# Second MLP of a two-layer decoder trunk: normed input and 512-column products from the twelfth output tile on; attention: matmul bursts of a pair merged with the next pair's

## The chip, the cores and the metric

The kernel runs on one NeuronCore of one Trainium2 chip. It is a single program. The metric is the device time of one execution in microseconds (us); lower is better. Everything is float32; many matrix products take operands in a rounded float32 format that the kernel calls F32R and that TensorE streams faster.

## The reference, cut to what matters

```python
# D_MODEL = 1024, SEQ = 256, BATCH = 1, H = 16 heads of 64, D_FF = 4096, two layers
for i in range(2):
    sh1, sc1, g1, sh2, sc2, g2 = split(silu(c) @ w_mod[i] + b_mod[i], 6)
    h = rmsnorm(x, norm_mix[i]) * (1 + sc1) + sh1
    y = pool_mixer(h) if i == 0 else moba_attention(h)   # one key block here: causal attention + bias
    x = x + g1 * y
    h = rmsnorm(x, norm_mlp[i]) * (1 + sc2) + sh2
    x = x + g2 * (relu(h @ w_up[i]) ** 2) @ w_down[i]
return rmsnorm(x, norm_final)
```

rmsnorm(x, g) is x * R * g, with R one number for each of the 256 positions.

## The kernel before, in words

**Layout.** Activations are kept transposed: a tile is 128 features by S = 256 positions, and x is eight such tiles `xs[k]`. A weight matrix is cut into 128x128 tiles; `w_all` in HBM holds all of them in the order of use, 16 to a chunk of 1 MB.

**Products in two parts.** Each weight tile is split into a rounded high part and the remainder: ACT (ScalarE) makes `w_hi` (`split_hi`, line 248, 128x1024 for eight tiles, a *half*), then DVE (VectorE) makes `w_lo` = raw - high (`split_lo`, line 258). Activations are split in the same way. A product is high x high + high x low + low x high. `mm_sum` (lines 277 to 279) does it in three matmuls of 256 or 258 columns. `mm_wide` (lines 270 and 271) does it in two: one of 512 columns, with high and low of the activation side by side, and one of 256, and leaves two half sums in one PSUM bank, 256 columns each, that have to be added.

**Steps.** PE (TensorE) takes one weight tile in a step. `next_tile` first runs what `later(d, fn)` put down for this step, then, at every eighth step, splits the half that is AHEAD = 3 halves ahead. Each engine works strictly in the order in which instructions were issued this way. The second MLP's halves are w96 to w127; at its step 8h half w(96+h+3) is split, so w105 is for output tile 9 and w107 for output tile 11.

**The second MLP's first product** (`up(1, raws, R)`, tiles named m1u0 to m1u31, 256 steps). The norm factor R comes only after the sub-layer has begun, so the input is not normed: `unnormed` makes x times gain, split, in tiles `h11_raw` with two more columns that hold the shift, and the products are 258 columns wide. Behind the product, `unnormed_out` (lines 471, 473) multiplies by R and adds up the two extra columns into a bias, both on DVE; then ACT does Relu with that bias (738), the square is on DVE for the first four outputs (740) and on ACT after that (742), ACT makes the high part (758), and DVE the low part seven steps later (762). The first four outputs are worked on together (32 steps, k first), each later one takes eight steps. R is made from the norm's sums at step 18 (`norm_tail`, N3_AT) and is there at about step 28 (`to_sbuf`, line 429). The second product of an MLP (`down`, m0d and m1d) uses `mm_wide` for seven of its eight outputs.

**Attention.** Eight pairs of heads. A pair p has three outputs of the qkv product, eight steps each; beside those run, at steps set by `later`: `scores` (tiles sc, line 976), then on DVE the logits, on ACT exp (1002) and `normalize` (line 1013, tiles L), then on PE three transposes for each head (`transposes`, tiles pt, line 1019), two transposes of the values (`values`, tile pv, line 1029) and the products with them (`outputs`, tile po, lines 1043, 1044). A burst of these stands between two steps of the qkv product.

## Time and profile before

| | |
|---|---|
| median of 3 runs | 544.37 us (544.1 to 544.8) |
| the profiled execution | 544.81 us, of which the span from first to last instruction is 543.0 us |
| busy: PE, weight loads, DVE, ACT | 532.2, 494.2, 413.2, 323.9 us |
| qkv product with attention beside it, first start of a qkv matmul to that of the next product (wo) | 232.7 to 324.0 us |
| wo product | 324.0 to 349.7 us |
| second MLP, first product (m1u) | 349.7 to 444.1 us |
| second MLP, second product (m1d) | 444.1 to 534 us |
| HBM read | 138.64 MB |

A row of the timeline gives start and duration in us, engine, source line, operation, output<-inputs, their shapes and the count; in brackets stands the idle time of the engine ahead of it and who ended it. A row of groups gives busy time in us and the mean of one in ns. "Released by" is inferred from semaphores. In the chain of waits the time of a piece reaches to the start of the next piece, so there it is the true spacing of matmuls, while a matmul's own duration (280 ns) overlaps the next one's.

### The profile page before, as it was taken

What the parts mean: (1) busy time and instruction counts of PE and PEld (TensorE: products, weight loads), DVE (VectorE), ACT (ScalarE), POOL (GpSimd) and SP (SyncE); (2) the same over time, 40 slices, a digit from 0 to 9 for tenths busy, and PEclk for the clock granted to TensorE, in tenths of its full rate; (3) what the DMA queues carried; (4) which work ended last, traced back from release to release, by engine and by line L of the source; (5) the groups of instructions that cost most, each with busy time, mean ns of one, the idle gap of its engine ahead of it and who ended that gap; (6) DMA issues with size and microseconds to landing.
All of it is one profiled execution on the core that took longest, in us unless ns stands there. A gap on an engine that the chain in (4) does not pass through costs nothing.

```text
span 543.0 us, 10968 instructions
## 1 busy us (share of the span) xinstructions
PE 532.2 (98%) x4412; PEld 494.2 (91%) x4412; DVE 413.2 (76%) x837; ACT 323.9 (60%) x606; POOL 2.5 (0%) x18
## 2 busy tenths in 40 slices
PE   8899999999999999999999999999999999999995
PEld 7777999999988888999998999999999998888895
DVE  2857997899889889857999983876887786775542
ACT  4225336788644545447987777657987874445531
POOL 1000000000000000000000000000000000000000
PEclk9999999999999999999999999999999999999998
DMA  8999998488899989964467774444565467676002
GB/s 331 422 415 418 419 416 313 156 308 320 314 381 406 364 304 336 341 238 148 185 236 298 278 275 156 156 156 156 185 215 198 179 237 281 211 273 240 0 1 77
DMA packets 22338, 140.41 MB, mean 259 GB/s; under 512 B 2416, under 2 KB 4736, under 8 KB 5904
## 3 DMA queue, kind: packets, MB, share of 16 engines
q1 hardware_dynamic: 22048, 138.61, 68.1%
q10 hardware_dynamic: 144, 1.05, 0.5%
q8 instruction: 34, 0.56, 0.4%
q14 instruction: 16, 0.13, 0.1%
q0 software_dynamic: 96, 0.06, 0.0%
HBM read 138.64 MB, written 1.07 MB: 257 GB/s over the span
## 4 chain that ended last, share of the span: by engine, by line
PE 92%; DMA 6%; DVE 1%; ACT 0%; issue 0%; DVEq 0%; ACTq 0%
PE m1d L270 10%; PE m0d L270 9%; PE m1u L277 6%; PE m1u L278 6%; PE m1u L279 6%; PE m0u L277 5%; PE m0u L279 5%; PE m0u L278 5%; PE m1d L271 5%; PE m0d L271 5%; PE qkv L277 5%; PE qkv L278 4%; PE qkv L279 4%; DMA raw_c_sh<-in_w_mod 3%; DMA raw_c_g<-in_w_mod 2%; PE wo L277 1%
## 5 line engine op out<-in xcount | busy, mean ns | idle before, releaser
L258 DVE TENSOR_TENSOR w_lo<-raw_w,w_hi 128x1024 fp32r<-128x1024 f32 x160 | 194.6, 1223 | 59.7 <-ACT w_hi L248 58.0
L248 ACT CAST w_hi<-raw_w 128x1024 fp32r<-128x1024 f32 x159 | 165.4, 1047 | 78.1 <-PE m1d L270 25.0
L270 PE MATMUL m1d<-m1u_al,w_hi 128*128 128x512 f32 x224 | 78.7, 394 | 0.0
L270 PE MATMUL m0d<-m0u_al,w_hi 128*128 128x512 f32 x224 | 78.1, 392 | 0.0
L301 DVE SCALAR_TENSOR_TENSOR raw_m<-raw_m,cact 128x1024 f32<-128x1024 f32 x64 | 77.6, 1217 | 0.0
L277 PE MATMUL m1u<-h_raw,w_hi 128*128 128x258 f32 x256 | 72.8, 284 | 0.0
L278 PE MATMUL m1u<-h_raw,w_hi 128*128 128x256 f32 x256 | 72.6, 284 | 0.0
L279 PE MATMUL m1u<-h_raw,w_lo 128*128 128x258 f32 x256 | 72.5, 283 | 0.0
L277 PE MATMUL m0u<-h,w_hi 128*128 128x256 f32 x248 | 69.8, 281 | 0.0
L279 PE MATMUL m0u<-h,w_lo 128*128 128x256 f32 x248 | 69.6, 281 | 0.0
L278 PE MATMUL m0u<-h,w_hi 128*128 128x256 f32 x248 | 69.4, 280 | 0.0
L271 PE MATMUL m1d<-m1u_al,w_lo 128*128 128x256 f32 x224 | 63.0, 281 | 0.0
L271 PE MATMUL m0d<-m0u_al,w_lo 128*128 128x256 f32 x224 | 62.8, 280 | 0.0
L277 PE MATMUL qkv<-h_raw,w_hi 128*128 128x258 f32 x192 | 57.4, 299 | 0.0
L278 PE MATMUL qkv<-h_raw,w_hi 128*128 128x256 f32 x192 | 54.5, 284 | 0.0
L279 PE MATMUL qkv<-h_raw,w_lo 128*128 128x258 f32 x192 | 54.4, 283 | 0.0
L270 PEld LDWEIGHTS m1d<-m1u_al,w_hi 128*128 128x128 f32 x224 | 42.1, 188 | 9.8
L270 PEld LDWEIGHTS m0d<-m0u_al,w_hi 128*128 128x128 f32 x224 | 42.0, 188 | 9.5
L279 PEld LDWEIGHTS m1u<-h_raw,w_lo 128*128 128x128 f32 x256 | 48.8, 191 | 0.0
L277 PEld LDWEIGHTS m1u<-h_raw,w_hi 128*128 128x128 f32 x256 | 48.7, 190 | 0.0
L278 PEld LDWEIGHTS m1u<-h_raw,w_hi 128*128 128x128 f32 x256 | 48.5, 190 | 0.0
L277 PEld LDWEIGHTS m0u<-h,w_hi 128*128 128x128 f32 x248 | 46.7, 188 | 0.6 <-issue 0.4
(189 smaller groups left out, 984.7 us busy)
## 6 DMA issues: line engine op xcount, KB each, us to landing
raw_w<-in_w_all SPq DMA_DIRECT2D x79, 1024.0 KB, 5.6
raw_m<-in_w_mod SPq DMA_DIRECT2D x32, 1024.0 KB, 6.4
raw_c_sh<-in_w_mod SPq DMA_DIRECT2D x8, 1024.0 KB, 14.1
raw_c_g<-in_w_mod SPq DMA_DIRECT2D x4, 1024.0 KB, 12.4
raw_c_mlp<-in_w_mod SPq DMA_DIRECT2D x2, 1024.0 KB, 11.6
raw_c_shift<-in_w_mod SPq DMA_DIRECT2D x2, 1024.0 KB, 9.1
T<-bd SPq DMA_DIRECT2D x8, 256.0 KB, 8.3
x<-in_xT ACTq DMA_DIRECT2D x1, 1024.0 KB, 5.7
```

The lines of the kernel that those rows point to most:

```text
L248: nc.scalar.copy(hi, raw)
L258: nc.vector.tensor_sub(lo, raw, hi.bitcast(F32))
L270: nc.tensor.matmul(b, hi, hl[:, : 2 * S], start=start, stop=False)
L271: nc.tensor.matmul(b[:, S:], lo, hl[:, :S], start=False, stop=stop)
L277: nc.tensor.matmul(dst, hi, xh, start=start, stop=False)
L278: nc.tensor.matmul(dst[:, :S], hi, xl, start=False, stop=False)
L279: nc.tensor.matmul(dst, lo, xh, start=False, stop=stop)
L301: nc.vector.scalar_tensor_tensor(raw[:, a], raw[:, a], 1.0, cact, op0=ALU.mult, op1=ALU.mult, accum_out=dst[:, a : a + 1])
```

## The change

Two edits.

**Second MLP.** Once R is there, eight normed input tiles `h11_0` to `h11_7` are made: at step 30 + 6k DVE computes u = x * gain * R, ACT adds the shift and rounds (high part), and two steps later DVE makes the low part. Output tiles 11 to 31 then use `mm_wide` on these; their two half sums are joined by an ACT copy and a DVE add in place of `unnormed_out`, and Relu has no bias. The first eleven outputs stay as they were.

**Attention.** Both heads' transposes of a pair are done at the step at which the next pair's scores are (24 steps after the pair's own scores, before: 25 and 26). For pairs 0 to 5, `outputs` is done at the head of the next pair's `values`, before: 9 steps after both inputs were issued.

```diff
+N_NORMED, NORMED_AT, NORMED_GAP = 11, 30, 6
+
+OUTPUTS_BESIDE = NP - 2
...
-    def up(layer, hl, R):
+    def up(layer, hl, R, normed=None):
...
+                elif n >= N_NORMED:
+                    u = tmp.tile([P, S], F32, tag="u", bufs=5, name=f"{nm}_u")
+                    nc.scalar.activation(u, banks[n][:, S:], AF.Copy)
+                    nc.vector.tensor_add(u, banks[n][:, :S], u)
                 else:
                     u, b = unnormed_out(banks[n], R[0], nm)
...
-                if R is not None:
+                if b is not None:
                     nc.scalar.activation(u, u, AF.Relu, bias=b)
+                elif R is not None:
+                    nc.scalar.activation(u, u, AF.Relu)
...
+            elif n >= N_NORMED:
+                mm_wide(banks[n], w, normed[k], k == 0, k == KD - 1)
...
-            later(25, lambda: self.transposes(0))
-            later(26, lambda: self.transposes(1))
+            for e in range(2):
+                later(24, lambda e=e: self.transposes(e))
...
         def values(self):
             p = self.p
+            if 0 < p <= OUTPUTS_BESIDE:
+                pairs[p - 1].outputs()
...
-            if self.v is not None and len(self.PT) == 2:
+            if self.v is not None and len(self.PT) == 2 and self.p >= OUTPUTS_BESIDE:
                 later(9 if self.p < NP - 1 else 5, self.outputs)
...
+    def normed_tile(k):
+        u = tmp.tile([P, S], F32, tag="h", bufs=2, name=f"h11_u{k}")
+        nc.vector.scalar_tensor_tensor(u, xs[k], gs11[:, k : k + 1], R[0], op0=ALU.mult, op1=ALU.mult)
+        t = normed[k] = act.tile([P, 2 * S], F32R, tag="T", bufs=NP, name=f"h11_{k}")
+        sh = modv(1, 3, k)[:, k : k + 1]
+        nc.scalar.activation(t[:, :S], u, AF.Identity, bias=sh)
+        later(
+            2,
+            lambda: nc.vector.scalar_tensor_tensor(
+                t[:, S:], u, sh, t[:, :S].bitcast(F32), op0=ALU.add, op1=ALU.subtract
+            ),
+        )
+
+    for k in range(KD):
+        later(NORMED_AT + NORMED_GAP * k, lambda k=k: normed_tile(k))
+    al = up(1, raws, R, normed)
```

**What moves on ACT.** In the second MLP's first product, between the weight half w104 and the weight half w105 (for output tiles 8 and 9), ACT had these rows before; m1u*N*_u is output N behind its product, m1u*N*_al its split result.

```order
L248 CAST w104_hi_4752<-raw_w_52_4374 128x1024
L738 ACTIVATE m1u4_u_4748<-m1u4_u_4748,m1u4_b_4750 128x256
L742 ACTIVATE m1u4_u_4748<-m1u4_u_4748 128x256
L758 CAST m1u4_al_4762<-m1u4_u_4748 128x256
L738 ACTIVATE m1u2_u_4783<-m1u2_u_4783,m1u2_b_4785 128x256
L758 CAST m1u2_al_4793<-m1u2_u_4783 128x256
L248 CAST w105_hi_4799<-raw_w_52_4374 128x1024
```

The same stretch of ACT now (line 252 is the former 248, 746 the former 738, 752 the former 742, 768 the former 758).

```order
L252 CAST w104_hi_4762<-raw_w_52_4374 128x1024
L746 ACTIVATE m1u4_u_4758<-m1u4_u_4758,m1u4_b_4760 128x256
L752 ACTIVATE m1u4_u_4758<-m1u4_u_4758 128x256
L768 CAST m1u4_al_4772<-m1u4_u_4758 128x256
L1115 ACTIVATE h11_2_4779<-h11_u2_4777,mod1_3_123 128x256
L1115 ACTIVATE h11_3_4807<-h11_u3_4805,mod1_3_123 128x256
L746 ACTIVATE m1u2_u_4798<-m1u2_u_4798,m1u2_b_4800 128x256
L768 CAST m1u2_al_4812<-m1u2_u_4798 128x256
L252 CAST w105_hi_4818<-raw_w_52_4374 128x1024
```

Two normed tiles' high parts now stand ahead of output 2's Relu and of the weight half w105.

**What moves on DVE** in the same stretch. Before:

```order
L258 TENSOR_TENSOR w104_lo_4754<-raw_w_52_4374,w104_hi_4752 128x1024
L762 TENSOR_TENSOR m1u1_al_4743<-m1u1_u_4734,m1u1_al_4743 128x256
L471 TENSOR_TENSOR m1u2_u_4783<-m1u2_4574,n3_R_4686 128x256
L473 TENSOR_REDUCE m1u2_b_4785<-m1u2_4574 128x1
L762 TENSOR_TENSOR m1u4_al_4762<-m1u4_u_4748,m1u4_al_4762 128x256
L740 TENSOR_TENSOR m1u2_u_4783<-m1u2_u_4783 128x256
L471 TENSOR_TENSOR m1u5_u_4795<-m1u5_4756,n3_R_4686 128x256
L473 TENSOR_REDUCE m1u5_b_4797<-m1u5_4756 128x1
L258 TENSOR_TENSOR w105_lo_4801<-raw_w_52_4374,w105_hi_4799 128x1024
```

The same stretch of DVE now:

```order
L262 TENSOR_TENSOR w104_lo_4764<-raw_w_52_4374,w104_hi_4762 128x1024
L1112 SCALAR_TENSOR_TENSOR h11_u2_4777<-x_82,gs1_4_4181,n3_R_4686 128x256
L1118 SCALAR_TENSOR_TENSOR h11_2_4779<-h11_u2_4777,mod1_3_123,h11_2_4779 128x256
L772 TENSOR_TENSOR m1u1_al_4753<-m1u1_u_4743,m1u1_al_4753 128x256
L475 TENSOR_TENSOR m1u2_u_4798<-m1u2_4574,n3_R_4686 128x256
L477 TENSOR_REDUCE m1u2_b_4800<-m1u2_4574 128x1
L1112 SCALAR_TENSOR_TENSOR h11_u3_4805<-x_82,gs1_4_4181,n3_R_4686 128x256
L772 TENSOR_TENSOR m1u4_al_4772<-m1u4_u_4758,m1u4_al_4772 128x256
L750 TENSOR_TENSOR m1u2_u_4798<-m1u2_u_4798 128x256
L475 TENSOR_TENSOR m1u5_u_4814<-m1u5_4766,n3_R_4686 128x256
L477 TENSOR_REDUCE m1u5_b_4816<-m1u5_4766 128x1
L262 TENSOR_TENSOR w105_lo_4820<-raw_w_52_4374,w105_hi_4818 128x1024
```

The first part and the low part of normed tile 2 stand next to each other, with ACT's high part of the same tile between them; the first part of tile 3 stands ahead of output 2's square.

**What moves on PE** in the attention, around pair 2's transposes (pt2) and pair 3's scores (sc3), two steps into the qkv output qkv4_0. Before:

```order
L976 MATMUL sc3_0_3463<-qk3_3342 128x128
L976 MATMUL sc3_1_3464<-qk3_3342 128x128
L976 MATMUL sc3_0_3463<-qk3_3342 128x256
L976 MATMUL sc3_1_3464<-qk3_3342 128x256
L277 MATMUL qkv4_0_3449<-h10_raw2_2343,w75_hi_3252 128x258
L278 MATMUL qkv4_0_3449<-h10_raw2_2343,w75_hi_3252 128x256
L279 MATMUL qkv4_0_3449<-h10_raw2_2343,w75_lo_3254 128x258
L1019 MATMUL pt2_0_3474<-vec_80,L2_0_3278 128x128
L1019 MATMUL pt2_0_3474<-vec_80,L2_1_3279 128x128 x2
```

And now (988 is the former 976, 1032 the former 1019):

```order
L1032 MATMUL pt2_0_3458<-vec_80,L2_0_3278 128x128
L1032 MATMUL pt2_0_3458<-vec_80,L2_1_3279 128x128 x2
L1032 MATMUL pt2_1_3463<-vec_80,L2_0_3278 128x128
L1032 MATMUL pt2_1_3463<-vec_80,L2_1_3279 128x128 x2
L988 MATMUL sc3_0_3468<-qk3_3347 128x128
L988 MATMUL sc3_1_3469<-qk3_3347 128x128
L988 MATMUL sc3_0_3468<-qk3_3347 128x256
L988 MATMUL sc3_1_3469<-qk3_3347 128x256
```

Pair 2's six transposes now stand ahead of pair 3's scores, at the same step. The products of pair 1 (po1), which stood one step ahead of sc3 before, stand at pair 2's values now, behind this place.

More of the change, by code (lines that the diff above doesn't have):

```diff
@@ L1092, in tile_hybrid_pool_moba @@
     norm_tail(rms, R, N3_AT)
-    al = up(1, raws, R)
+    normed = [None] * KD
+    def normed_tile(k):
[13 more added lines that the diff above has]
+    al = up(1, raws, R, normed)
     rms = Rms("nf")
```

## The prediction

> **What bounds the kernel now.** I read the page first, then the chain of waits, then the tile view of the three MLP products that are compared below.
>
> ```profile
> PE 532.2 (98%) x4412; PEld 494.2 (91%) x4412; DVE 413.2 (76%) x837; ACT 323.9 (60%) x606; POOL 2.5 (0%) x18
> PE 92%; DMA 6%; DVE 1%; ACT 0%; issue 0%; DVEq 0%; ACTq 0%
> ```
>
> PE is busy for 98% of the span and makes 92% of the chain that ended last. From the first MLP on, nothing else stands on the chain: a matmul that gets shorter there shortens the kernel, and a wait of PE lengthens it. So the change is a sum over PE's stream: what its matmuls save, less what PE is newly made to wait.
>
> ```profile
> L277 PE MATMUL m1u<-h_raw,w_hi x256: 277/283/367, 349.7 to 443.7; 128*128 128x258 f32 x128
> L270 PE MATMUL m1d<-m1u_al,w_hi x224: 388/394/403, 444.1 to 522.5; 128*128 128x512 f32 x112
> L270 PE MATMUL m0d<-m0u_al,w_hi x224: 387/393/402, 143.2 to 221.0; 128*128 128x512 f32 x112
> ```
>
> ```profile
> 356.42 0.79 PE n_rms L396 x8
> 360.94 0.70 PE n_rms L421 x4
> ```
>
> The first fence gives the first and last start of each kind. In m1u 255 steps take 94.0 us, less 1.6 for the two norm bursts (the chain's 0.79 and 0.70, and 0.11 on the matmul behind the first): 0.3624 us a step. A wide step takes 78.4/223 = 0.3516 in m1d and 77.8/223 = 0.3489 in m0d.
>
> **Wide products: -1.8 us.** Outputs 11 to 31 are 21 x 8 = 168 steps. At m1d's rate each saves 0.0108, together 1.8 us; at m0d's 0.0135, 2.3. I take m1d's, since its place is next. The Trainium skill, page "TensorE: Matmul & The Clock Gate", section "Back-to-back issue gap", gives N/2.4 + 2.5 ns for a matmul of N columns; by it, as an estimate, the step would save only 4 ns and the edit 0.7 us. The rows say 11 to 14 ns, and I keep to them.
>
> **What joins the halves: 0.** For each of the 21 outputs the multiplication by R (DVE) becomes a copy from PSUM on ACT and an add on DVE, the 150 ns reduction goes, and Relu loses its bias.
>
> ```profile
> L471 DVE TENSOR_TENSOR m1u_u<-m1u,n_R 128x256 f32<-128x256 f32 x32 | 13.5, 421 | 2.7 <-PE m1u L279 2.6
> L731 ACT ACTIVATE m0u_u<-m0u 128x256 f32<-128x256 f32 x18 | 6.8, 379 | 5.1 <-PE m0u L279 5.1
> L668 DVE SCALAR_TENSOR_TENSOR h_u<-x,gs,n_R 128x256 f32<-128x256 f32 x6 | 2.6, 482 | 0.1
> L674 ACT ACTIVATE h<-h_u,mod 128x256 fp32r<-128x256 f32 x8 | 3.8, 504 | 14.7 <-DVE pk L331 11.0 <-DVE h_u L668 3.7
> L677 DVE SCALAR_TENSOR_TENSOR h<-h_u,mod,h 128x256 fp32r<-128x256 f32 x8 | 3.6, 483 | 1.0 <-ACT h L674 1.0
> ```
>
> ACT gains a copy like L731's (0.38). Where ACT and DVE are behind, the trace has them turning out one output in 2.29 us (382.98 less 380.69, below), against 2.81 for eight wide steps; with the copy it is some 2.5 to 2.7. PE's eight steps hide that; without that cover it would be at most 21 x 0.38 = 8 us, and I take 0.
>
> **Normed tiles: +6.8 us.** This decides. Eight times DVE 0.48, ACT 0.50, DVE 0.48 (the last three rows, the same operations in the first MLP), 11.8 us if nothing overlapped, are put between steps 30 and 74. Into what?
>
> ```profile
> 365.03 1.23 DVE L258 TENSOR_TENSOR w_lo<-raw_w,w_hi 128x1024 fp32r<-128x1024 f32 x1 [1.43 <-ACT w_hi L248]
> 369.42 1.23 DVE L258 TENSOR_TENSOR w_lo<-raw_w,w_hi 128x1024 fp32r<-128x1024 f32 x1 [1.02 <-ACT w_hi L248]
> 373.81 1.23 DVE L258 TENSOR_TENSOR w_lo<-raw_w,w_hi 128x1024 fp32r<-128x1024 f32 x1 [1.02 <-ACT w_hi L248]
> 376.42 1.22 DVE L258 TENSOR_TENSOR w_lo<-raw_w,w_hi 128x1024 fp32r<-128x1024 f32 x1
> 380.69 1.23 DVE L258 TENSOR_TENSOR w_lo<-raw_w,w_hi 128x1024 fp32r<-128x1024 f32 x1
> 382.98 1.23 DVE L258 TENSOR_TENSOR w_lo<-raw_w,w_hi 128x1024 fp32r<-128x1024 f32 x1
> ```
>
> These are the low parts of w103 to w108. Step 8h of m1u begins at 349.73 + 8h x 0.3624 + 1.6, and its first low product stands 0.24 later: 377.66 for w105 (h = 9), 380.56 for w106, 383.46 for w107. They are ready at 375.04, 377.64 and 381.92, so PE's lead is 2.6, 2.9 and only 1.5 us. It has melted since w103, though neither engine is full: they wait for each other.
>
> ```profile
> 361.68 0.37 ACT L429 COPY n_R<-n_rms 128x256 f32<-128x256 f32 x1 [1.16 <-PE n_rms L421]
> 367.02 0.51 ACT L738 ACTIVATE m1u_u<-m1u_u,m1u_b 128x256 f32<-128x256 f32 x1 [2.03 <-DVE m1u_b L473]
> 368.34 1.05 ACT L248 CAST w_hi<-raw_w 128x1024 fp32r<-128x1024 f32 x1
> 371.41 0.51 ACT L738 ACTIVATE m1u_u<-m1u_u,m1u_b 128x256 f32<-128x256 f32 x1 [0.73 <-DVE m1u_b L473]
> 372.73 1.04 ACT L248 CAST w_hi<-raw_w 128x1024 fp32r<-128x1024 f32 x1
> ```
>
> ACT idles 2.03 us for an output's bias, DVE 1.02 to 1.43 us for a weight's high part, and the next weight part stands behind in each queue. A normed tile is one more such exchange, DVE to ACT to DVE. I walked the new order by hand with these durations, next instruction 0.08 us before the end of the one ahead where independent (as the rows are spaced), a hand-over 0.03, from R at 361.68 on. Tile 0 moves w104's split by 0.8, tile 1 makes it 1.13. Then, behind w104's low part: first part of tile 2 0.40, DVE idle 0.65 for ACT's high part, low part 0.40, first part of tile 3 0.40, its high part on ACT 0.41. Output 2's Relu, at 371.41 now, comes 1.13 + 2.26 = 3.4 us later, and w105's split stands behind it: its low part starts at 377.2 instead of 373.81. In the same way w106's starts at 381.0 (tile 4) and w107's at 386.2 (tile 5), w107's high part at 384.6, and tile 7's low part ends at 392.4.
>
> PE therefore waits 0.8 at step 72 (378.4 for 377.7), 0.9 at step 80, 0.8 and 1.55 at step 88 for w107's high and low part, and, six wide steps further on at 389.7, 2.75 for input tile 7: 6.8 us. Behind that the lead grows again. Bounds: 0 if the tiles fit into the idle times above, and 11.8 less the 1.5 of lead, 10, if nothing overlaps. I take 6.8 because the walk goes through the queues as they stand.
>
> **Attention: +1.1 us.** Is a merged burst cheaper?
>
> ```profile
> 267.00 0.33 PE pt L1019 x3
> 267.33 0.59 PE po L1043 x4
> 267.92 0.22 PE po L1044 x4
> 268.14 0.32 PE qkv L277
> ...
> 277.98 0.22 PE pv L1029 x2
> ...
> 281.46 0.59 PE po L1043 x4
> 282.05 0.22 PE po L1044 x4
> 282.27 0.32 PE qkv L277
> ```
>
> At 267 transposes and products already stand in one burst: 0.33 + 0.59 + 0.22, and 0.32 for the qkv matmul behind. At 281 the products alone cost 0.59 + 0.22 and the same 0.32. Three transposes cost 0.33, two 0.22, in any company: no fixed part to save. Only the 0.2 on the matmul behind the products could go, where transposes now follow them: six times, -1.2 at the very most; +0 is what the rows show, and I take 0.
>
> Both transposes of pair 2 are earlier, and the products of pair 1 no longer stand ahead of them.
>
> ```profile
> 272.20 0.76 PE L1043 MATMUL po<-PT,v 128*64 128x256 f32 x4
> 273.66 0.93 PE L976 MATMUL sc<-qk 64*128 64x128 f32 x8
> 293.01 0.66 PE L1043 MATMUL po<-PT,v 128*64 128x256 f32 x4
> 296.92 0.93 PE L976 MATMUL sc<-qk 64*128 64x128 f32 x8
> ```
>
> ```profile
> 272.56 1.50 ACT L1013 ACTIVATE L<-L,rs 128x128 f32<-128x128 f32 x4
> ...
> 295.40 0.37 ACT L1048 CAST ol<-po 128x256 fp32r<-128x256 f32 x1
> 295.65 0.52 ACT L1013 ACTIVATE L<-L,rs 128x256 f32<-128x256 f32 x1
> ```
>
> po ahead of the scores at 273.66 took 0.59 + 0.22 + 0.20 = 1.0, and 0.1 of waiting (0.76 against 0.66 at 293.01). Without it PE comes at 272.5 and would be through six transposes at 273.1. The last two need the fourth normalization, which ends at 274.06: they end at 274.3, 1.2 later. Less the old 0.1, net +1.1; bounds 0 (ACT ahead) and 1.7 (the earlier transposes wait one by one too). Queued behind them is pair 3's sc burst. From pair 3 on I count no wait: pair 4's fourth normalization ends at 296.17, or 295.9 without the cast of po ahead of it, and PE, coming 1.0 before 296.92, needs it at the fifth transpose, 296.4. Were these 0.5 gone, four pairs would cost some 0.3 each, 1.2.
>
> **The sum.** -1.8 + 0 + 6.8 + 0 + 1.1 = +6.1. The profiled execution took 544.81 (span 543.0, 1.8 around it), so 550.9; it stands 0.44 above the median 544.37, against which the forecast is 550.5.
>
> **Rivals.** (1) The exchanges overlap: a normed tile delays the splits by no more than one issue, 0.41. Four tiles ahead of w105 make 1.6 and five ahead of w106 2.1, inside their leads; six ahead of w107 make 2.5, 0.9 over its lead, and two more tiles 0.3. Sum +1.2 - 1.8 + 1.1 = +0.5: 544.9. For it speak the idle times; against it that they are caused by the order itself, which the new rows lengthen. (2) Faster: ACT and DVE take all eight tiles in their idle times. It decides at w107: if less than 1.5 us is added ahead of it, PE never waits; half of the 1.2 above and the saving are left: -0.6 - 1.8 = -2.4, 542.0, or 542.5 without the merging. Against it: one exchange of tile 2 alone shows 1.05 of DVE time with ACT idle around it. (3) The waits slow PE's clock.
>
> ```profile
> 537.00:540.00 3.00, 0.00 (x0) 0.00 (x0) 1.61 (x4) 1.26 (x2) 0.00 (x0) 1.00 0.48 177
> 540.00:543.00 3.00, 0.00 (x0) 0.00 (x0) 0.00 (x0) 0.00 (x0) 0.00 (x0) 0.54 0.44 172
> ```
>
> With PE idle from 537 the granted clock stayed 1.00 for 3 us, then averaged 0.54. The longest wait that I walk is 2.75, so it should hold; if it falls for 3 us, 0.46 x 3 = 1.4 is added: 551.9. The Trainium skill, same page, "Why this matters for your kernels", warns of PE gaps above some 3 us between bursts; by that rule the last wait is just short of trouble. That the edits don't happen is no case: the rows of the new order show them.
>
> **How the numbers follow.** Forecast 0.73, 550.5; (1) 0.11, 544.9; (2) 0.08, 542; (3) 0.08, 551.9. About 0.2% (1.1 us) is what a measurement of this kernel can tell from no change. The forecast and (3) are slower, (1) half same and half slower: faster 0.08, same 0.06, slower 0.86. The range leaves out (2) and most of (1) and goes from waits of some 2 us (546) to 552.7, with more serial exchanges and the slower clock.
>
> **What would show it.** Right: idle time of PE ahead of m1u matmuls between 376 and 394, released by DVE w_lo, ACT w_hi and h11, about 7 us; wide m1u steps of 0.35; PE waiting over 1 us for ACT once at pt2; low parts of w105 to w107 3 to 6 us later than now. Wrong: m1u shorter than 94.4 us without PE idle, or bursts of po and pv below 1.2 us.

## The result and the profile after

The changed kernel took 549.76 us, the median of six runs (548.64 to 553.11), against 544.77 for the kernel before (six runs, 544.1 to 545.02): the ratio is 1.0104, with a 95% interval of 1.0072 to 1.0136. It is 5.0 us slower; 550.5 was forecast. The profiled execution was the longest of the six, 553.11 us with a span of 551.3, against 544.81 and 543.0 before, so the trace has 8.3 us to account for, 3.3 more than the medians.

From the page of the changed kernel: the busy time of PE, the granted clock in 40 slices of 13.8 us, and the chain that ended last.

```profile
PE 536.6 (97%) x4244; PEld 488.2 (89%) x4244; DVE 417.8 (76%) x832; ACT 331.0 (60%) x635; POOL 2.5 (0%) x18
PEclk9999999999999999999999999999699999999999
PE 81%; DVE 9%; ACT 5%; DMA 2%; issue 2%; DVEq 0%; ACTq 0%
```

PE fell from 92% of the chain to 81%; DVE (9%, before 1%) and ACT (5%, before 0) stand on it now. And one slice, number 29, shows a clock of six tenths: it spans 386 to 400 us, in m1u. To place the loss by stage, the tile views give the first and last starts: first qkv of the kernel before (its m1u and m1d rows stand in the prediction), then qkv, m1u and m1d of the changed kernel (x88 are the 258-column steps, x168 the wide ones).

```profile
L277 PE MATMUL qkv<-h_raw,w_hi x192: 277/283/393, 232.7 to 323.6; 128*128 128x258 f32 x192
```

```profile
L281 PE MATMUL qkv<-h_raw,w_hi x192: 277/282/393, 232.7 to 323.1; 128*128 128x258 f32 x192
L281 PE MATMUL m1u<-h_raw,w_hi x88: 276/283/367, 350.3 to 385.3; 128*128 128x258 f32 x88
L274 PE MATMUL m1u<-h,w_hi x168: 387/398/766, 386.3 to 452.5; 128*128 128x512 f32 x168
L274 PE MATMUL m1d<-m1u_al,w_hi x224: 387/392/403, 452.9 to 530.7; 128*128 128x512 f32 x112
```

From the start of qkv to that of m1u: 117.6 us against 117.0, so attention costs 0.6. m1u: 102.6 (350.3 to 452.9) against 94.4, so +8.2. The wide part of m1d: 77.8 against 78.4, so -0.6, in a stage that the change doesn't touch. Now PE's rows in m1u that begin behind idle time (the bracket: us idle, and what ended it):

```profile
379.09 0.39 PE L283 MATMUL m1u<-h_raw,w_lo 128*128 128x258 f32 x1 [0.73 <-DVE w_lo L262]
382.88 0.39 PE L283 MATMUL m1u<-h_raw,w_lo 128*128 128x258 f32 x1 [0.61 <-DVE w_lo L262]
386.31 0.50 PE L274 MATMUL m1u<-h,w_hi 128*128 128x512 f32 x1 [0.52 <-ACT w_hi L252]
388.09 0.39 PE L275 MATMUL m1u<-h,w_lo 128*128 128x256 f32 x1 [1.29 <-DVE w_lo L262]
393.17 0.77 PE L274 MATMUL m1u<-h,w_hi 128*128 128x512 f32 x1 [1.50 <-DVE h L1118]
```

Five waits, at steps 72, 80, 88 (twice) and 95, for just the operands that the forecast named: w105's low part, w106's low part, w107's high and low part, normed tile 7. The brackets are smaller than what PE loses, since the modelled end of a matmul runs past the start of the next. By the spacing of starts (0.362 us a step, measured on the 81 undisturbed 258-column steps) the first four lose 0.99, 0.87, 0.68 and 1.65, together 4.2. What DVE did meanwhile: the low parts of w105 to w107, and the low half of normed tile 7.

```profile
377.81 1.23 DVE L262 TENSOR_TENSOR w_lo<-raw_w,w_hi 128x1024 fp32r<-128x1024 f32 x1 [1.02 <-ACT w_hi L252]
381.61 1.22 DVE L262 TENSOR_TENSOR w_lo<-raw_w,w_hi 128x1024 fp32r<-128x1024 f32 x1
386.82 1.22 DVE L262 TENSOR_TENSOR w_lo<-raw_w,w_hi 128x1024 fp32r<-128x1024 f32 x1
392.54 0.48 DVE L1118 SCALAR_TENSOR_TENSOR h<-h_u,mod,h 128x256 fp32r<-128x256 f32 x1
```

Counted from m1u's start (350.28 here, 349.73 before) the three splits begin at 27.53, 31.33 and 36.54; the walk had 377.2, 381.0 and 386.2, which are 27.5, 31.3 and 36.5. Tile 7 is complete at 42.74; the walk had 42.7. The queues went as walked.

And the clock, in stretches of 3 us (columns: PE, PEld, DVE, ACT, POOL busy with counts, PEclk, DMA share, GB/s):

```profile
385.00:388.00 3.00, 1.28 (x8) 0.77 (x6) 2.65 (x7) 2.25 (x5) 0.00 (x0) 1.00 0.00 0
388.00:391.00 3.00, 2.91 (x12) 2.53 (x13) 2.05 (x7) 1.92 (x4) 0.00 (x0) 0.69 0.62 191
...
394.00:397.00 3.00, 3.00 (x11) 2.52 (x11) 2.55 (x5) 2.90 (x6) 0.00 (x0) 0.50 0.31 82
...
400.00:403.00 3.00, 3.00 (x19) 2.59 (x18) 2.54 (x5) 2.94 (x7) 0.00 (x0) 1.00 0.63 210
```

Behind the two waits at step 88 (PE busy for 1.28 of 3 us) the clock fell to 0.50 and stayed there until about 399 (0.61 from 397 to 400). Between 394 and 397 eleven matmuls started where 19 do at full clock; single wide steps follow each other at 0.64 us instead of 0.35, a step's other matmul included:

```profile
394.59 0.63 PE L274 MATMUL m1u<-h,w_hi 128*128 128x512 f32 x1
...
395.23 0.63 PE L274 MATMUL m1u<-h,w_hi 128*128 128x512 f32 x1
```

The spacing of the wide steps adds up so: 0.8 for the slow steps up to 391, 2.0 ahead of tile 7's step, 2.9 for the slow steps behind it. With the first four waits that is 9.8; 168 wide steps at 0.3532 (mean of the 152 undisturbed ones) save 168 x 0.0091 = 1.5; the difference, 8.3, is the stage's +8.2 within the rounding.

In attention, PE's rows at pair 2's transposes, at pair 3's, which do not wait, and one of the new bursts of po and pv with its neighbours:

```profile
272.30 0.29 PE L283 MATMUL qkv<-h_raw,w_lo 128*128 128x258 f32 x1
272.63 0.33 PE L1032 MATMUL pt<-vec,L 128*128 128x128 f32 x1
273.32 0.84 PE L1032 MATMUL pt<-vec,L 128*128 128x128 f32 x5 [0.36 <-ACT L L1026]
274.09 0.93 PE L988 MATMUL sc<-qk 64*128 64x128 f32 x8
...
277.45 0.28 PE L283 MATMUL qkv<-h_raw,w_lo 128*128 128x258 f32 x1
277.66 0.66 PE L1058 MATMUL po<-PT,v 128*64 128x256 f32 x4
...
278.47 0.44 PE L1044 MATMUL pv<-vec,vT 128*128 128x128 f32 x2
...
278.87 0.28 PE L282 MATMUL qkv<-h_raw,w_hi 128*128 128x256 f32 x1
...
284.78 0.29 PE L283 MATMUL qkv<-h_raw,w_lo 128*128 128x258 f32 x1
284.90 0.82 PE L1032 MATMUL pt<-vec,L 128*128 128x128 f32 x6
285.65 0.93 PE L988 MATMUL sc<-qk 64*128 64x128 f32 x8
```

From the qkv matmul ahead of the six transposes to the scores behind them it is 0.87 us at pair 3 (284.78 to 285.65), where PE needn't wait, and 1.79 at pair 2 (272.30 to 274.09), so pair 2 loses 0.9 to its normalizations on ACT. The burst of po and pv costs 278.87 - 277.45 less two qkv spacings of 0.12, so 1.18; apart, the same spacing gives 1.01 and 0.22 in the kernel before. Six such bursts save 0.3, and the old wait ahead of po is gone: 0.9 - 0.3 - 0.1 is the stage's 0.5 to 0.6.

### The profile page after: what moved, and what is told of

Its sections match the earlier page's. It is cut to its first block, busy times and chain, and to the rows that moved or that the text cites. A ratio compares the mean times of both kernels' runs of the same rounds, so it can differ in the third digit from the quotient of the medians.

```text
span 551.3 us, 10682 instructions
## 1 busy us (share of the span) xinstructions
PE 536.6 (97%) x4244; PEld 488.2 (89%) x4244; DVE 417.8 (76%) x832; ACT 331.0 (60%) x635; POOL 2.5 (0%) x18
## 4 chain that ended last, share of the span: by engine, by line
PE 81%; DVE 9%; ACT 5%; DMA 2%; issue 2%; DVEq 0%; ACTq 0%
PE m1d L274 9%; PE m0d L274 9%; PE m1u L274 7%; PE m0u L281 5%; PE m0u L283 5%; PE m0u L282 5%; PE m0d L275 5%; PE m1d L275 5%; PE qkv L281 4%; PE m1u L275 4%; PE qkv L282 3%; PE qkv L283 3%; DVE w_lo L262 3%; DMA raw_c_g<-in_w_mod 2%; PE junk L353 2%
## 5 line engine op out<-in xcount | busy, mean ns | idle before, releaser
L274 PE MATMUL m1d<-m1u_al,w_hi 128*128 128x512 f32 x224 | 78.2, 393 | 0.0
L274 PE MATMUL m1u<-h,w_hi 128*128 128x512 f32 x168 | 63.3, 418 | 2.0 <-DVE h L1118 1.5
L281 PE MATMUL qkv<-h_raw,w_hi 128*128 128x258 f32 x192 | 55.9, 291 | 0.0
L275 PE MATMUL m1u<-h,w_lo 128*128 128x256 f32 x168 | 49.0, 292 | 1.3 <-DVE w_lo L262 1.3
L281 PEld LDWEIGHTS m0u<-h,w_hi 128*128 128x128 f32 x248 | 46.7, 188 | 0.6 <-issue 0.4
L283 PEld LDWEIGHTS m0u<-h,w_lo 128*128 128x128 f32 x248 | 46.7, 188 | 0.2 <-DVE w_lo L262 0.2
L282 PEld LDWEIGHTS m0u<-h,w_hi 128*128 128x128 f32 x248 | 46.7, 188 | 0.0
L274 PEld LDWEIGHTS m1u<-h,w_hi 128*128 128x128 f32 x168 | 33.4, 199 | 11.0 <-ACT m1u_al L768 2.0
L275 PEld LDWEIGHTS m1d<-m1u_al,w_lo 128*128 128x128 f32 x224 | 42.1, 188 | 0.0
```

The costliest lines, as they stand in the source:

```text
L274: nc.tensor.matmul(b, hi, hl[:, : 2 * S], start=start, stop=False)
L275: nc.tensor.matmul(b[:, S:], lo, hl[:, :S], start=False, stop=stop)
L281: nc.tensor.matmul(dst, hi, xh, start=start, stop=False)
L282: nc.tensor.matmul(dst[:, :S], hi, xl, start=False, stop=False)
L283: nc.tensor.matmul(dst, lo, xh, start=False, stop=stop)
```

## The experiments

The theory behind them: the normed tiles are eight more hand-overs between DVE and ACT, these two already wait for each other at that place, and the parts of three weights come too late for PE; the wide products pay 1.5 to 2 us back; attention costs little; the clock's fall comes on top because PE stood still. The rivals: the joins or the wide products make the waits; attention has the larger part; the clock fell for another reason. The first four kernels take the change apart.

**The MLP edit alone.** Both attention edits are undone.

```diff
-            for e in range(2):
-                later(24, lambda e=e: self.transposes(e))
+            later(25, lambda: self.transposes(0))
+            later(26, lambda: self.transposes(1))
...
-            if 0 < p <= OUTPUTS_BESIDE:
-                pairs[p - 1].outputs()
...
-            if self.v is not None and len(self.PT) == 2 and self.p >= OUTPUTS_BESIDE:
+            if self.v is not None and len(self.PT) == 2:
```

> The MLP edit alone: normed tiles and wide products as in the changed kernel, attention's bursts as before. Theory (normed tiles make PE wait some 6 us ahead of the last steps up to 94 of m1u, wide products give 1.8 back, the rest of the loss is the clock): the changed kernel's 549.8 less the 0.55 us by which its stages up to the second MLP were longer in the trace, so about 549.2, ratio to before 1.008, with m1u's five waits all there. Rival, attention's edit is the larger part: 545 to 547. Rival, the attention edit really saves: more than 549.8.

Measured: 550.85 us (549.97 to 551.59), ratio 1.0112 (1.0098 to 1.0126). The loss is all here, and the attention edit is not the larger part. The value is 1.7 over the theory's, and by the number alone the second rival, an attention edit that really saves (more than 549.8), is met. The interval lies inside that of the whole change, however, and the next run has attention at 0.0, so the 1.3 us between this kernel (four executions) and the changed one (six, 4.5 us apart) stays open. The profiled execution was the shortest, 549.97. Its m1u is 5.4 us longer than before, the five waits are there, and the clock fell to 0.50 behind step 88 again, for 3.4 us; but here the slow steps only used up time in which PE would have waited for tile 7 (slow steps and that wait together lose 2.8), so the fall cost next to nothing.

**The attention edit alone.** The second MLP is as before.

```diff
-N_NORMED, NORMED_AT, NORMED_GAP = 11, 30, 6
+N_NORMED, NORMED_AT, NORMED_GAP = 99, 30, 6
...
-    for k in range(KD):
+    for k in range(0):
         later(NORMED_AT + NORMED_GAP * k, lambda k=k: normed_tile(k))
```

> The attention edit alone: merged bursts, second MLP as before. Theory: the wait of PE for the fourth normalization of pair 2 (0.9 us with the transposes in one burst) less 0.05 us for each of six merged bursts of products and values, +0.55 as the trace had it: 545.3, ratio 1.001. The forecast's term was +1.1: 545.9. Rival, merged bursts pay: 544.0 or less. Rival, attention carries most of the loss: 548 or more.

Measured: 544.53 us (544.21 to 544.97), ratio 1.0 (0.9991 to 1.0009): no change, under the theory's 545.3 and the forecast's 545.9. The tile views say why:

```profile
L281 PE MATMUL qkv<-h_raw,w_hi x192: 277/283/393, 232.6 to 323.0; 128*128 128x258 f32 x192
L281 PE MATMUL m1u<-h_raw,w_hi x256: 276/283/367, 350.1 to 444.2; 128*128 128x258 f32 x128
L274 PE MATMUL m1d<-m1u_al,w_hi x224: 387/392/403, 444.5 to 522.4; 128*128 128x512 f32 x112
```

qkv to m1u is 117.5, +0.5 as in the changed kernel; m1d's 224 wide steps take 77.9 instead of 78.4, -0.5. The second is an effect that nobody forecast; more on it below.

**The wide products and the joins alone.** Outputs 11 to 31 go over the unnormed input tiles, and no normed tile is made; attention as before. The kernel leaves out the norm and the shift of these outputs.

```diff
-                mm_wide(banks[n], w, normed[k], k == 0, k == KD - 1)
+                mm_wide(banks[n], w, t, k == 0, k == KD - 1)
...
-    for k in range(KD):
+    for k in range(0):
         later(NORMED_AT + NORMED_GAP * k, lambda k=k: normed_tile(k))
```

> The wide products and the joining of their halves alone: outputs 11 to 31 are made of the unnormed input tiles in 512-column products, and no normed tile is made; the norm and the shift of these outputs are left out. Attention as before. Theory: 168 steps save 0.0108 us each by the rows of before, 0.010 by those of the changed kernel, and the copy and the add stay beside PE's work: -1.7 to -1.8, 543.0, ratio 0.9968, no PE wait over 0.3 us in m1u. Rival, the copy on ACT and the add on DVE make the weight parts late: PE waits in m1u for w_lo as in the changed kernel, 547 to 549. Rival, the smaller price of the wide product by the gap of the Trainium skill's page on matmul: -0.7, 544.1.

Measured: 542.58 us (542.21 to 542.68), ratio 0.996 (0.9947 to 0.9972): -2.0. The wide products pay, and the 21 joins (a copy on ACT and an add on DVE each) cost nothing: the trace has no wait of PE in m1u at all.

```profile
L274 PE MATMUL m1u<-h_raw,w_hi x168: 388/396/426, 382.8 to 441.2; 128*128 128x512 f32 x168
```

58.4 us for 167 steps are 0.350 a step; the saving of 0.7 us, the prediction's estimate from the gap that the Trainium skill gives (page "TensorE: Matmul & The Clock Gate", section "Back-to-back issue gap"), is outside the interval.

**The normed tiles alone.** All eight are made at the same steps, but no product reads them, and outputs 11 to 31 are joined as before.

```diff
-                elif n >= N_NORMED:
+                elif n >= KF:
                     u = tmp.tile([P, S], F32, tag="u", bufs=5, name=f"{nm}_u")
...
-            elif n >= N_NORMED:
+            elif n >= KF:
                 mm_wide(banks[n], w, normed[k], k == 0, k == KD - 1)
```

> The normed tiles alone: all eight are made at the same steps as in the changed kernel, and nothing uses them; all products of m1u go over the unnormed tiles as before, attention as before. Theory: the tiles' exchanges between DVE and ACT make w105 to w107 late, PE waits 1 + 0.9 + 0.7 + 1.7 us as in the changed kernel, less the wait for the last normed tile itself (1.7), which nothing needs now: +4 to +4.5, 549, ratio 1.008; more if the clock falls behind the waits (up to +8). Rival, the wait comes from the wide products or the joins: 544.8, ratio 1.000.

Measured: 550.64 us (550.47 to 551.0), ratio 1.0108 (1.0092 to 1.0123): +6.05, without any change to what PE computes. That decides between theory and rival, and it is 1.5 over the theory's value for full clock. PE's waits in m1u, the second and third of six left out:

```profile
378.88 0.39 PE L283 MATMUL m1u<-h_raw,w_lo 128*128 128x258 f32 x1 [0.73 <-DVE w_lo L262]
...
387.88 0.39 PE L283 MATMUL m1u<-h_raw,w_lo 128*128 128x258 f32 x1 [1.28 <-DVE w_lo L262]
391.21 0.39 PE L281 MATMUL m1u<-h_raw,w_hi 128*128 128x258 f32 x1 [0.40 <-ACT w_hi L252]
392.47 0.39 PE L283 MATMUL m1u<-h_raw,w_lo 128*128 128x258 f32 x1 [0.75 <-DVE w_lo L262]
```

The first four are those of the changed kernel (by spacing 0.99, 0.88, 0.67, 1.65). The last two, for w108's high and low part, 0.6 and 1.1 by spacing, are new: in the changed kernel PE is held up by normed tile 7 in that time, so w108 comes early enough. The sum is 5.9, and the clock stayed at 1.00 throughout.

The single parts add up: 6.05 for making the tiles, 1.0 more because PE waits 2.7 for tile 7 (measured below) in place of 1.7 for w108, -2.0 for the wide products and 0.0 for attention are +5.1, against +5.0 for the whole change.

The next two kernels test the clock. **Products of a constant in place of idleness**, ahead of step 88, in the changed kernel; they go to output 11's bank and are overwritten at once. Each of the five shows as two rows of PE.

```diff
+            if normed is not None and n == N_NORMED and k == 0:
+                for _ in range(5):
+                    nc.tensor.matmul(banks[n][:, :S], ident, xs[0], start=True, stop=True)
```

> The changed kernel with five products of a constant tile (256 columns, fp32, 0.43 us each; their result is overwritten at once) put on PE ahead of step 88 of m1u, where the changed kernel's PE otherwise idles some 2.3 us: no wait for data is taken away, only the idleness. Theory (the granted clock falls because PE idles in several places in a few us): no stretch of m1u below clock 1.00 behind step 88, no steps of 0.64, runs within 1 us of each other, at 544.6 + 4.2 (waits ahead of steps 72 to 88) + 1.5 (wait for normed tile 7) - 2.2 (wide products) + 0 (attention) = 548.1. Rival, the clock falls because of the wide products or by chance: stretches at 0.5 as before, median 549 to 551, runs 4 us apart. Rival, the products cost their own time: up to 550.3 with the clock at 1.00.

Measured: 550.33 us (549.97 to 551.18), ratio 1.0104 (1.009 to 1.0117). In the profiled execution the fall at step 88 is gone, and the four executions are 1.2 us apart instead of 4.5; but a fall came behind the next wait.

```profile
386.02 2.32 PE L790 MATMUL m1u<-x,vec 128*128 128x256 f32 x10
...
390.44 0.40 PE L274 MATMUL m1u<-h,w_hi 128*128 128x512 f32 x1
...
393.52 0.47 PE L274 MATMUL m1u<-h,w_hi 128*128 128x512 f32 x1 [2.57 <-DVE h L1121]
```

```profile
391.00:394.00 3.00, 0.48 (x3) 0.47 (x4) 2.25 (x5) 2.90 (x5) 0.00 (x0) 1.00 0.51 216
394.00:397.00 3.00, 3.00 (x14) 2.58 (x14) 2.55 (x7) 2.76 (x6) 0.00 (x0) 0.65 0.21 46
```

With PE at full speed the step of normed tile 7 waits 2.57 us (3.08 from start to start, 2.73 more than a step); in the changed kernel's trace it was 1.50 only because the slow clock had used up the rest. The expectation had taken that 1.5 for the undisturbed size, which is 1.1 of the 2.2 us by which it was low; the slow steps behind the wait, 1.6 us in this trace, more than make up the rest.

**The same with six more such products ahead of step 95**, where tile 7 is waited for.

```diff
-                banks[n] = banks[n - 1] if paired else bank(f"{name}{n}")
+                banks[n] = banks[n - 1] if paired else banks.get(n) or bank(f"{name}{n}")
...
+            if normed is not None and n == N_NORMED and k == KD - 1:
+                banks[n + 1] = bank(f"{name}{n + 1}")
+                for _ in range(6):
+                    nc.tensor.matmul(banks[n + 1][:, :S], ident, xs[0], start=True, stop=True)
```

> As the kernel with five products of a constant ahead of step 88, and six more of them (2.6 us, into the bank of the next output, overwritten) ahead of step 95, where PE otherwise waits 2.6 us for normed tile 7. No data comes earlier; only PE's idleness goes. Theory (idleness brings the fall of the clock): clock 1.00 all through m1u, no step of 0.64, time 544.8 + 6.8 (waits, filled or not) - 2.2 (wide products) + 0 (attention) = 549.4, runs within 1 us. Rival, the clock falls behind these places whatever PE does, or by the wide products: stretches at 0.5 to 0.8 again and 550.3 or more.

Measured: 549.38, 549.01 and 550.41 us, beside one execution (the profiled one) of 1845.27, in which PE was busy for 1838 us, with the granted clock given as 1.00 and DVE and ACT busy no longer than usual (427 and 337 us), for a reason that its trace doesn't show, and which says nothing on m1u; ratio of the others 1.0093 (1.0078 to 1.0109). The two shorter ones fit the theory's 549.4, the third the rival's 550.3 or more. Without a trace of an ordinary execution this stays inconclusive.

**Used one output later.** The MLP edit alone, with `N_NORMED = 12` instead of 11: the tiles are made at the same steps, and step 95 needs none.

> The MLP edit alone, normed tiles made at the same steps, but used from output 12 on: output 11 stays in 258-column products, so step 95 no longer needs normed tile 7. Theory: the wait for that tile goes (it is there 42.7 us behind m1u's start, needed at 45), the waits for weight parts stay as where the tiles were made and not used (0.99 + 0.88 + 0.67 + 1.65 + 0.58 + 1.12 = 5.9), 160 steps save 0.0131 each, 2.1: +3.8, 548.6. The clock: where the same idleness at step 88 was followed by 258-column products, it stayed at 1.00; if the wide ones behind it are what brings it down, it stays here at 1.00 until step 96 and may fall behind that (up to +2); if it was chance, it may fall behind step 88. Rival, the wait for tile 7 just moves into another: 549.8 as the MLP edit alone.

Measured: 548.91 us (547.62 to 549.45), ratio 1.0075 (1.0062 to 1.0087), within 0.3 of the theory. No wait for a normed tile is left. On the clock it says that the fall needs no wide products:

```profile
385.00:388.00 3.00, 1.28 (x7) 1.07 (x8) 2.57 (x6) 2.12 (x5) 0.00 (x0) 0.97 0.00 0
388.00:391.00 3.00, 3.00 (x16) 3.00 (x15) 2.08 (x6) 2.02 (x5) 0.00 (x0) 0.50 0.89 309
```

Here the same idleness as where the tiles were only made was followed by the same 258-column products, and the clock fell to 0.50, while there it stayed at 1.00. (The slow steps, 1.7 us, then took the place of the waits for w108, 0.6 and 1.1, so the total is the expected one.)

Two more kernels split the attention edit. **Merged transposes only:**

```diff
-            if 0 < p <= OUTPUTS_BESIDE:
-                pairs[p - 1].outputs()
...
-            if self.v is not None and len(self.PT) == 2 and self.p >= OUTPUTS_BESIDE:
+            if self.v is not None and len(self.PT) == 2:
```

(second MLP as before here and in the next.)

> Half of the attention edit: both heads' transposes in one burst, the products of po where they were, second MLP as before. Theory: pair 2's burst waits for its fourth normalization as in the changed kernel, +0.9, no other saving: up to m1u +0.9; the whole 545.5 with m1d at its old 0.3513 us a step, 545.0 if m1d runs at 0.3489 as in the kernels with the whole attention edit (224 x 0.0024 = 0.5). Rival, merged transposes are cheaper: 544 or less up to m1u.

Measured: 544.16 us (543.82 to 544.42), ratio 0.9987 (0.9978 to 0.9996): -0.6, where the theory had +0.2 to +0.7. Its premise failed: there is no wait at pair 2.

```profile
273.42 0.82 PE L1032 MATMUL pt<-vec,L 128*128 128x128 f32 x6
274.17 0.93 PE L988 MATMUL sc<-qk 64*128 64x128 f32 x8
```

With pair 1's po still ahead of them (from 271.43 on) the transposes begin at 273.42, 0.8 us later than in the changed kernel, and it is 0.75 us from their start to the scores, as at pair 3 (0.74): all four normalizations are done. From qkv to m1u it is 116.7, against 117.0; m1u is 94.6, against 94.4; m1d's wide part is 77.9 (below), against 78.4.

```profile
L281 PE MATMUL qkv<-h_raw,w_hi x192: 277/282/393, 232.6 to 323.4; 128*128 128x258 f32 x192
L281 PE MATMUL m1u<-h_raw,w_hi x256: 277/283/367, 349.3 to 443.6; 128*128 128x258 f32 x128
L274 PE MATMUL m1d<-m1u_al,w_hi x224: 387/393/400, 443.9 to 521.8; 128*128 128x512 f32 x112
```

**Products of po beside values only:**

```diff
-            for e in range(2):
-                later(24, lambda e=e: self.transposes(e))
+            later(25, lambda: self.transposes(0))
+            later(26, lambda: self.transposes(1))
```

> The other half of the attention edit: products of po beside the next pair's values, transposes apart as before, second MLP as before. Theory: six merged bursts at 1.18 instead of 1.01 + 0.22, -0.3, and the small wait ahead of po at 272 goes, -0.1; against that the products of pair 0, now right behind its second transposes, may wait for their copies to SBUF (0 to 1.6): 544.2 without that wait, up to 545.8 with it, each 0.5 less if m1d runs at 0.3489 us a step. Rival, moving po costs as much as the whole edit's +0.5 up to m1u: 545.1.

Measured: 545.95 us (545.74 to 546.48), ratio 1.0022 (1.0014 to 1.0031): +1.2, just over the upper end. The named wait is there, and long (0.90 in the bracket, 1.6 by spacing, the upper end of what was named):

```profile
263.13 0.49 PE L1032 MATMUL pt<-vec,L 128*128 128x128 f32 x3
265.60 0.65 PE L1058 MATMUL po<-PT,v 128*64 128x256 f32 x2 [0.90 <-ACT PT L1034]
```

So the halves don't add up (-0.6 and +1.2 against 0.0 together): pair 0's products stand right behind its transposes only if these come as late as before; in the whole edit the transposes come earlier, and the wait moves to pair 2's normalizations.

The last three look for a kernel that keeps the gain. **Normed tiles later and further apart**, attention as before:

```diff
-N_NORMED, NORMED_AT, NORMED_GAP = 11, 30, 6
+N_NORMED, NORMED_AT, NORMED_GAP = 22, 66, 14
```

> The MLP edit alone (attention as before) with the normed tiles made later and further apart, from step 66 of m1u on, one every 14 steps, and used from output 22 on. Theory (the tiles cost PE time only because several exchanges between DVE and ACT stand ahead of weight parts that have little lead): no PE wait over 0.3 us in m1u, 10 x 8 = 80 steps save 0.0131 each by the run of the wide products alone, 1.0: 543.6, ratio 0.998, clock at 1.00 throughout m1u. Rival, a normed tile costs its exchange wherever it stands (8 tiles, some 0.5 to 0.7 each): 547 to 549. Rival, eight tiles cost what little lead there is only once: some 545.

Measured: 543.67 us (543.55 to 544.33), ratio 0.998 (0.9971 to 0.9989), the theory's number. PE waits for no weight part in m1u, and once, 0.3 us by spacing, for normed tile 7, the bound that the theory had set. (The profiled execution was one of the longer, 544.23; its m1u is 0.5 us shorter than before, with wide steps of 0.353, so half of the gain is not in the trace.) The same eight tiles with the same operations cost next to nothing where they stand apart and at weights with lead. **Normed tiles on GpSimd**, attention as before, used from output 13:

```diff
-        nc.vector.scalar_tensor_tensor(u, xs[k], gs11[:, k : k + 1], R[0], op0=ALU.mult, op1=ALU.mult)
-        t = normed[k] = act.tile([P, 2 * S], F32R, tag="T", bufs=NP, name=f"h11_{k}")
+        nc.gpsimd.tensor_mul(u, xs[k], R[0])
         sh = modv(1, 3, k)[:, k : k + 1]
-        nc.scalar.activation(t[:, :S], u, AF.Identity, bias=sh)
...
+        nc.gpsimd.tensor_scalar(u, u, gs11[:, k : k + 1], sh, op0=ALU.mult, op1=ALU.add)
+        t = normed[k] = act.tile([P, 2 * S], F32R, tag="T", bufs=NP, name=f"h11_{k}")
+
+        def high():
+            nc.scalar.copy(t[:, :S], u)
+            nc.gpsimd.tensor_sub(t[:, S:], u, t[:, :S].bitcast(F32))
+
+        later(8, high)
```

> Attention as before; the normed tiles are made on GpSimd, which is idle there: it multiplies the input tile by R, scales and shifts, and subtracts the high half; ACT only copies the high half, DVE does nothing for them. Same first step and spacing, used from output 13 on, 19 x 8 = 152 wide steps. Theory (the loss comes from DVE's and ACT's exchanges alone): weight parts as early as before but for eight ACT copies of 0.4, no PE wait over 0.3 us, 152 x 0.0131 = 2.0 saved: 542.8, clock 1.00. Rival, GpSimd needs over 1.5 us a tile and operation, or slows DVE beside it: PE waits for normed tiles or w_lo, 546 to 552.

Measured: 546.45 us (546.29 to 546.84), ratio 1.0037 (1.0024 to 1.0051): the rival, at its low end. PE waits twice for w_lo (0.85 and 0.70 us in the brackets) and 0.2 for a tile, 2.5 together by spacing, with the clock at 1.00 throughout m1u. GpSimd's and DVE's groups:

```profile
L1117 POOL TENSOR_TENSOR h<-h_u,h 128x256 fp32r<-128x256 f32 x8 | 7.6, 955 | 6.5 <-ACT h L1116 6.5
...
L1112 POOL TENSOR_SCALAR h_u<-h_u,gs,mod 128x256 f32<-128x256 f32 x8 | 5.7, 717 | 0.8
...
L772 DVE TENSOR_TENSOR m1u_al<-m1u_u,m1u_al 128x256 fp32r<-128x256 f32 x32 | 16.0, 499 | 1.7 <-ACT m1u_al L768 1.2
```

GpSimd needs 0.7 to 0.96 us an operation, and DVE's low parts of the outputs take 499 ns in the mean against 424 before: single ones took 0.78 to 0.96 while GpSimd ran. So the work left DVE's queue, but still slowed DVE. **Both parts that paid**, tiles from step 66 and merged transposes:

```diff
-N_NORMED, NORMED_AT, NORMED_GAP = 11, 30, 6
+N_NORMED, NORMED_AT, NORMED_GAP = 22, 66, 14
...
-            if 0 < p <= OUTPUTS_BESIDE:
-                pairs[p - 1].outputs()
...
-            if self.v is not None and len(self.PT) == 2 and self.p >= OUTPUTS_BESIDE:
+            if self.v is not None and len(self.PT) == 2:
```

> The two parts that paid together: normed tiles from step 66 on, one every 14 steps, used from output 22 on, and both heads' transposes in one burst; the products of po where they were. Theory (the parts are independent): 544.7 - 1.1 (late tiles) - 0.6 (merged transposes) = 543.0, ratio 0.997. Rival, the gain of the merged transposes sits in another place of m1d's operands and is lost when the normed tiles take buffers too: 543.6.

Measured: 543.82 us (543.51 to 544.17), ratio 0.998 (0.9971 to 0.9989): faster than both kernels, but no faster than the late tiles alone. Its profile has the shorter stages of both: qkv to m1u 116.7, m1u 94.1 (against 94.4), m1d's wide steps 77.9. In the traces the parts do add up: -0.5 for the late tiles and -0.5 for the merged transposes alone, -1.0 from qkv's start to the end here, which is what the medians show. What is open is the 0.6 by which the late tiles' median gained more than their trace; the theory had counted on it.

## Why the prediction was right, point by point

**Wide products, -1.8:** right. 1.5 by the step's length in the changed kernel (0.3532 against 0.3623), 2.0 as measured alone. The step was not quite one number: 0.350 over the unnormed tiles, 0.353 over the normed ones, against 0.3516 taken from m1d.

**Joins, 0:** right, shown by the kernel with them and without normed tiles: no wait, -2.0.

**Normed tiles, +6.8:** right, in size and place. Making them is enough (+6.05). The four waits ahead of steps 72 to 88 were walked as 0.8, 0.9, 0.8, 1.55 and measured as 0.99, 0.87, 0.68, 1.65; the wait for tile 7 was walked as 2.75 and is 2.73 at full clock, in the kernel with products of a constant. The walked starts were met to within 0.1 us, because they were taken from the order of the two queues and the durations in the trace, and not from the shares in which DVE (76%) and ACT (60%) are busy: a quarter of the span on DVE, 130 us, is ten times the work of the tiles, and the late tiles show that there was room, only not there. Rival 1, exchanges that overlap, and rival 2, tiles in idle time, are refuted for this place by the same rows; for steps 66 to 164 rival 2 is what happened.

**Bursts, 0, and transposes, +1.1:** the stage up to m1u came out at +0.55, the edit as a whole at 0.0. Two steps failed. In "the fourth normalization, which ends at 274.06" the old time was kept; ACT's cast of po, which stood ahead of it, moved away with the products of po, and the normalizations ended 0.4 earlier, so the wait is 0.9 and not 1.2. The four normalizations now:

```profile
272.17 1.49 ACT L1026 ACTIVATE L<-L,rs 128x128 f32<-128x128 f32 x4
```

The second step is the bursts: a burst of po and pv costs 1.18, under the 1.2 that the prediction named as a sign of being wrong. It saves 0.05 six times, 0.3, where the forecast allowed up to 0.2 each and took none. The remaining -0.5 lies in m1d and was no step at all.

**The clock:** the step "The longest wait that I walk is 2.75, so it should hold" failed: rival 3, which had the chance 0.08 and the price 1.4, happened beside the forecast. In the profiled execution it cost about 2.9 (9.8 lost in m1u, of which 4.2 + 2.7 are waits at full clock); with the MLP edit alone it cost next to nothing. The runs spread from 548.6 to 553.1, where before they spread over 0.9; that this is the clock's doing is likely, but only one of the six was traced.

What the fall follows is shown in part. It came only where PE waited in m1u, but not wherever it did: the waits at step 88 were followed by it in three profiled executions and, with the normed tiles only made, by none in a fourth, and GpSimd's tiles made PE wait without it. So its absence at step 88 in the one traced execution with the products of a constant agrees with the theory, but may be chance. How long it lasts is plain: read in stretches of a quarter of a us, the clock was at 0.50 for 3.4 us with the MLP edit alone, used one output later and with the products of a constant, and for 10.2 us, three times that, in the changed kernel. The Trainium skill, page "TensorE: Matmul & The Clock Gate", section "What's actually happening", has an activity window of some 3.4 us that runs freely and isn't aligned to the program; these lengths agree with it, and so does a fall behind the same waits in one execution and none in another. The same page's "Why this matters for your kernels" sets the danger at PE gaps over some 3 us; here two gaps of 0.52 and 1.29 us in brackets, 2.3 us by spacing, with one matmul between them, were followed by the fall, and so was one of 2.57, so the measurement decides: gaps below 3 us aren't safe.

**The sum.** With the terms of the traces it is -1.5 + 0 + 6.9 + 0 = +5.4 at full clock, against +5.0 between the medians and +6.1 in the forecast. That the median came within 0.8 us of the forecast is partly luck: 1.1 was counted for attention, which cost nothing, the clock's fall wasn't in the sum, and single executions lie from 1.9 us under the forecast to 2.6 over it. With the fall the sum should be a little over 5.4. Three of the six runs, 548.6 to 549.0, lie 1.2 to 1.5 us under the 550.2 that 5.4 makes. One candidate is in the traces: in the kernel with products of a constant the undisturbed wide steps of m1u took 0.3472 us, in the changed kernel's profile 0.3532, and 168 x 0.006 is 1.0. That a run of the same program can have the one or the other was not shown; it stays open.

## What to carry to other kernels

Two engines that hand work to each other and idle in turn may have no spare time at that place, however low their busy shares (76% and 60% here): another hand-over moves everything behind it in both queues. Price it by walking the queues with the trace's durations against the lead of the consumer, and put such work where the lead is large and spread out; the same eight tiles cost 6 us at one place and 0.3 at another. A wait that is measured beside a slow clock is not its own size: it shrinks by what the slow steps used up (1.50 in the bracket with them, 2.57 without).

## What the hardware showed besides

- The same 512-column step over the same kind of operands differs by program: m1d's 224 steps took 78.3 to 78.4 us in every kernel with attention as before, 77.8 to 77.9 in every kernel with merged transposes, the MLP's edit in or out, and 78.2 with moved products of po alone. The cause is open; whether m1d's tiles and banks lie elsewhere there was not looked at.
- GpSimd beside DVE: a low half of 128x256 took 0.73 us on GpSimd at its shortest, and 1.46 and 1.74 in the two rows that begin during a split of DVE's; DVE's 0.42 rose to as much as 0.96 behind a start of GpSimd's. The Trainium skill, page "SBUF — State Buffer", section "Terms", has the two share a pair of ports, the loser waiting for a whole instruction; these rows agree.
- PE was idle for 3 us at the end of the kernel before with the granted clock at 1.00, and the clock fell behind idle times of 0.5 and 1.3 us in the middle of the changed one.
- A float32 product of 256 columns took 0.40 us of PE (the products of a constant), one in F32R 0.12.
